# FFN openings put in another order, and the banks of the down units copied out by ScalarE before VectorE adds them to the residual

## The chip, the cores and the metric

The kernel runs on one core of one Trainium2 chip. The metric is the device time of one execution in microseconds, the median of several runs. The engines are named as the profile names them: PE is TensorE (PEld its weight loads), DVE is VectorE, ACT is ScalarE, POOL is GpSimd, and SP is the queue that issues the weight transfers.

## What is computed

One encoder layer over 256 tokens of width 2048, in float32. Two feed-forward blocks (FFN1, FFN2, hidden width 5632) stand around a mixing block, and a small gated embedding and a last norm follow. The change touches the two feed-forward blocks only.

```python
def _rmsnorm(x, g):
    y = x32 * lax.rsqrt(jnp.mean(x32 * x32, axis=-1, keepdims=True) + RMS_EPS)
    return (y * g.astype(jnp.float32)).astype(x.dtype)
def _swiglu(x, wg, wu, wd):
    return (jax.nn.silu(x @ wg) * (x @ wu)) @ wd
...
  h = h + 1/2 * SwiGLU_1(RMSNorm(h))
  (mixing block: attention and short convolution, one output projection)
  h = h + 1/2 * SwiGLU_2(RMSNorm(h))
  h = h + sigmoid(RMSNorm(h) @ W_gate) * (p @ W_ple)
out = RMSNorm(h)
```

## The kernel before, in words

**Pieces.** The residual `h` lies in two token tiles of 128 rows. Weights come in pieces of 128 x 1024 floats, one transfer of 512 KB each on SP, into six `raw` buffers. Each piece is split into two parts whose sum is the weight: ACT writes `whi` (line 109, shown as L45, the line of the helper `act`), DVE writes `wlo` (line 110). Six such pairs of buffers exist (`HELD`, line 93). A product of two such split numbers is three matmuls (L114 to L116), so a piece is 12 matmuls of 128 x 512. A **unit** is the output of 512 columns for both token tiles: two banks of the accumulator memory under the tag `mm`. There are two `mm` banks, so the next such unit can start only when both banks of the unit before have been read out. In the down projection of the first hidden chunk (`down(0, 1, ...)`, names `d0_0` to `d0_3`) a unit is 2 pieces; in the later ones it is 4.

**Gate, up, down.** The hidden width is cut into 11 chunks of 512. `g0` and `u0` are gate and up of the first chunk, done with plain pieces. The other ten gate chunks are done in five **pairs** (`Pair`, names `ffn1s0` to `ffn1s4`) by a product scheme with seven products in place of eight. A pair has 12 steps. In steps 0 to 7 DVE first makes three sums of weights (L347 to L349) and then two pieces are split; steps 8 to 11 make two sums (L358) and split three pieces. The activation side of the scheme comes from `factors`: four small additions on DVE (L317 to L320, `sv`), a rounding on ACT (`sh`) and a difference on DVE (L322, `sl`), one call for each of 4 x 2 groups of 256 rows. After step 11 `whole` (line 402) copies one accumulator on ACT (`x`) and makes six sums on DVE (L405 to L410). `silu` on ACT, `after` (products with the up part on DVE, L486 and for pair 0 also L490) and `turn` (eight transposes on PE, names `gT1`, `gT2`, whose results ACT and DVE split again into `g1h`, `g1l`) follow through a queue.

**What sets the order.** `drive` writes the instructions of every engine in program order, and this order is kept. An item is a piece or a step. Its preparation (transfer, sums, split) is written up to six pieces ahead of its matmuls. `queue` holds deferred work, and `pump` writes one entry of it after each plain piece. `plain_stream` gives the plain pieces: `u0`, `u1`, `u2`, the four units of `down(0, ...)`, then `down` of two chunks and `ups` of two chunks in turn. `everything` puts the steps of the pairs between plain pieces: `at` (lines 556 and 563) says after how many plain pieces each of the 12 steps of pair 0 stands, and `base` where the later pairs begin. In `opening` FFN1 still lacks its `factors`, and calls one for each piece of `u0`; FFN2 has half of them and queues the other four, and its `rstd` behind them.

**The lines of the change.** `run` in `unit_items` (line 158) writes the matmuls, pumps one entry and then, at a unit's last piece, calls `done`. In `down` (line 511) `done` adds both banks, halved, to `h` on DVE (L516). In `up0` FFN1's `done` computes `rstd` (reduction at L225), applies it on ACT, and multiplies on DVE (L448, `gated`). In FFN2 the gate itself stays in the two `mm` banks until ACT's `ffn2sg` has read it.

## Time and profile before

| | |
|---|---|
| median of 3 runs | 1963.72 us (1963.34 to 1965.5) |
| profiled execution: its own time | 1965.0 us |
| its span, and mean granted clock of TensorE | 1962.9 us, 0.989 |
| busy: PE, DVE, ACT, POOL | 1910.3, 1473.9, 1056.6, 35.7 us |
| DMA | 437.09 MB, 65.7% of 16 engines' span |

The span is what the profiler covers of an execution, and the execution's own time stands 2.1 us above it. "Busy" is the share of time in which an engine has an instruction under way. A wait is a stretch in which an engine stands still until a semaphore comes from elsewhere. The granted clock is the share of its full speed that TensorE is given (its levels are 2.4 and 1.2 GHz, so 0.5 is the lower one). A timeline row gives the start, the duration, the engine, the line, the operation with its output and input, and in brackets how long the engine had been idle and what released it.

### The profile page before, as it was taken

What the parts mean: (1) busy time and instruction counts of PE and PEld (TensorE: products, weight loads), DVE (VectorE), ACT (ScalarE), POOL (GpSimd) and SP (SyncE); (2) the same over time, 40 slices, a digit from 0 to 9 for tenths busy, and PEclk for the clock granted to TensorE, in tenths of its full rate; (3) what the DMA queues carried; (4) which work ended last, traced back from release to release, by engine and by line L of the source; (5) the groups of instructions that cost most, each with busy time, mean ns of one, the idle gap of its engine ahead of it and who ended that gap; (6) DMA issues with size and microseconds to landing.
All of it is one profiled execution on the core that took longest, in us unless ns stands there. A gap on an engine that the chain in (4) does not pass through costs nothing.

```text
span 1962.9 us, 23890 instructions
## 1 busy us (share of the span) xinstructions
PE 1910.3 (97%) x8649; PEld 1578.6 (80%) x8649; DVE 1473.9 (75%) x1712; ACT 1056.6 (54%) x1345; POOL 35.7 (2%) x36
## 2 busy tenths in 40 slices
PE   8898999999999999999999989989999999999998
PEld 6686888888888888888888868868888888888887
DVE  6877978879788765656656668778797887987664
ACT  7554555555555555555445555545555555555653
POOL 0000000000000000100000000000000000000010
PEclk9998999999999999999999999989999999999999
DMA  8575776777767765555555547747777667777652
GB/s 293 196 259 186 265 265 225 264 251 245 266 223 240 270 201 183 192 172 165 177 190 177 187 163 230 273 163 260 253 244 271 222 239 268 240 269 238 204 182 99
DMA packets 127206, 437.09 MB, mean 223 GB/s; under 512 B 13808, under 2 KB 14320, under 8 KB 126832
## 3 DMA queue, kind: packets, MB, share of 16 engines
q1 hardware_dynamic: 127088, 435.57, 65.7%
q8 instruction: 68, 1.11, 0.2%
q14 instruction: 50, 0.41, 0.1%
HBM read 433.41 MB, written 2.10 MB: 222 GB/s over the span
## 4 chain that ended last, share of the span: by engine, by line
PE 92%; DVE 3%; ACT 3%; issue 1%; DMA 1%; POOL 0%; ACTq 0%; SPq 0%; POOLq 0%; DVEq 0%
PE ffn2u L114 4%; PE ffn2u L116 4%; PE ffn2u L115 4%; PE ffn1d L114 4%; PE ffn2d L114 4%; PE ffn1d L116 4%; PE ffn1d L115 4%; PE ffn2d L116 4%; PE ffn2d L115 4%; PE ffn1u L114 4%; PE ffn1u L116 4%; PE ffn1u L115 4%; PE o L114 1%; PE o L116 1%; PE o L115 1%; PE pg L116 1%
## 5 line engine op out<-in xcount | busy, mean ns | idle before, releaser
L45 ACT ACTIVATE whi_ffn1s<-raw_ffn1s 128x1024 fp32r<-128x1024 f32 x120 | 126.2, 1061 | 169.6 <-DVE raw_ffn1s L347 38.0
L45 ACT ACTIVATE whi_ffn2s<-raw_ffn2s 128x1024 fp32r<-128x1024 f32 x120 | 126.0, 1061 | 165.3 <-DVE raw_ffn2s L347 39.7
L110 DVE TENSOR_TENSOR wlo_ffn2s<-raw_ffn2s,whi_ffn2s 128x1024 fp32r<-128x1024 f32 x120 | 144.6, 1221 | 14.0 <-ACT whi_ffn2s L45 9.7
L110 DVE TENSOR_TENSOR wlo_ffn1s<-raw_ffn1s,whi_ffn1s 128x1024 fp32r<-128x1024 f32 x120 | 144.7, 1221 | 11.1 <-ACT whi_ffn1s L45 6.5
L114 PE MATMUL ffn2u<-whi_ffn2u,aTh 128*128 128x512 f32 x352 | 138.5, 393 | 7.4 <-ACT ffn2sg L45 7.4
L114 PE MATMUL ffn1u<-whi_ffn1u,aTh 128*128 128x512 f32 x352 | 139.3, 396 | 5.7 <-DVE ffn1sg L448 3.4
L115 PE MATMUL ffn1u<-wlo_ffn1u,aTh 128*128 128x512 f32 x352 | 138.7, 394 | 4.0 <-DVE wlo_ffn1u L110 4.0
L110 DVE TENSOR_TENSOR wlo_ffn2u<-raw_ffn2u,whi_ffn2u 128x1024 fp32r<-128x1024 f32 x88 | 106.0, 1221 | 43.6 <-ACT whi_ffn2u L45 42.4
L116 PE MATMUL ffn1u<-whi_ffn1u,aTl 128*128 128x512 f32 x352 | 138.1, 392 | 0.0
L115 PE MATMUL ffn2u<-wlo_ffn2u,aTh 128*128 128x512 f32 x352 | 137.7, 391 | 0.0
L116 PE MATMUL ffn2u<-whi_ffn2u,aTl 128*128 128x512 f32 x352 | 137.7, 391 | 0.0
L110 DVE TENSOR_TENSOR wlo_ffn1u<-raw_ffn1u,whi_ffn1u 128x1024 fp32r<-128x1024 f32 x88 | 105.7, 1221 | 38.2 <-ACT whi_ffn1u L45 37.2
L45 ACT ACTIVATE whi_ffn2u<-raw_ffn2u 128x1024 fp32r<-128x1024 f32 x88 | 91.1, 1055 | 63.9 <-PE ffn2u L116 45.0
L110 DVE TENSOR_TENSOR wlo_ffn2d<-raw_ffn2d,whi_ffn2d 128x1024 fp32r<-128x1024 f32 x88 | 104.9, 1219 | 17.4 <-ACT whi_ffn2d L45 17.2
L45 ACT ACTIVATE whi_ffn1u<-raw_ffn1u 128x1024 fp32r<-128x1024 f32 x88 | 90.7, 1054 | 50.5 <-PE ffn1u L116 40.8
L110 DVE TENSOR_TENSOR wlo_ffn1d<-raw_ffn1d,whi_ffn1d 128x1024 fp32r<-128x1024 f32 x88 | 104.7, 1220 | 12.4 <-ACT whi_ffn1d L45 12.0
L45 ACT ACTIVATE whi_ffn2d<-raw_ffn2d 128x1024 fp32r<-128x1024 f32 x88 | 89.3, 1048 | 16.3 <-PE ffn2d L116 8.0
L45 ACT ACTIVATE whi_ffn1d<-raw_ffn1d 128x1024 fp32r<-128x1024 f32 x88 | 89.2, 1048 | 11.3 <-PE ffn1d L116 5.1
L114 PEld LDWEIGHTS ffn1u<-whi_ffn1u,aTh 128*128 128x128 f32 x352 | 66.6, 189 | 21.9 <-ACT whi_ffn1u L45 4.4
L114 PEld LDWEIGHTS ffn2u<-whi_ffn2u,aTh 128*128 128x128 f32 x352 | 66.6, 189 | 21.4 <-ACT ffn2sg L45 7.8
L115 PEld LDWEIGHTS ffn1u<-wlo_ffn1u,aTh 128*128 128x128 f32 x352 | 66.8, 190 | 19.6 <-DVE wlo_ffn1u L110 6.0
L116 PEld LDWEIGHTS ffn1u<-whi_ffn1u,aTl 128*128 128x128 f32 x352 | 66.7, 189 | 13.8
(809 smaller groups left out, 5108.9 us busy)
## 6 DMA issues: line engine op xcount, KB each, us to landing
raw_ffn1s<-in_ws SPq DMA_DIRECT2D x120, 512.0 KB, 5.5
raw_ffn2s<-in_ws SPq DMA_DIRECT2D x120, 512.0 KB, 5.4
raw_ffn1u<-in_wu SPq DMA_DIRECT2D x88, 512.0 KB, 5.1
raw_ffn1d<-in_wd SPq DMA_DIRECT2D x88, 512.0 KB, 4.9
raw_ffn2u<-in_wu SPq DMA_DIRECT2D x88, 512.0 KB, 5.1
raw_ffn2d<-in_wd SPq DMA_DIRECT2D x88, 512.0 KB, 4.8
raw_o<-in_wout SPq DMA_DIRECT2D x32, 512.0 KB, 4.5
raw_pg<-in_wpg SPq DMA_DIRECT2D x24, 512.0 KB, 4.6
```

Of the source, the lines that this page charges most:

```text
L45: nc.scalar.activation(out=out, in_=in_, func=func, **kw)
L110: tt(out=lo[:, sl], in0=raw[:, sl], in1=f(hi[:, sl]), op=ALU.subtract)
L114: nc.tensor.matmul(ps, lhsT=xh, rhs=wh, start=first, stop=False)
L115: nc.tensor.matmul(ps, lhsT=xh, rhs=wl, start=False, stop=False)
L116: nc.tensor.matmul(ps, lhsT=xl, rhs=wh, start=False, stop=last)
```

## The change

`down` no longer adds from the banks, except in the last chunk: ACT copies each bank into a work tile (`o`), and the addition on DVE goes into a list `soon`, which `run` empties after the matmuls of the next plain piece, ahead of `done` and of the pumped entry. `done` now comes before the pump, and the number of entries to pump is fixed before it. In all 20 units of each feed-forward block are copied, 80 copies of 128 x 512. FFN1's eight `factors` are spread over `u0` and `u1`, one for every second piece. Both tables `at` are new. The queue entry between `after` and `turn` is left out for FFN1's pair 0, and the second half of `after` of pair 0 becomes an entry of its own. In FFN2 `rstd` stands ahead of the four `factors` in the queue.

```diff
@@ -116,6 +116,7 @@
         nc.tensor.matmul(ps, lhsT=xl, rhs=wh, start=False, stop=last)
 
     queue = deque()
+    soon = []
 
     def pump(n=1):
         for _ in range(min(n, len(queue))):
@@ -162,9 +163,12 @@
                 banks["wide"] = wide
                 st["ps"] = unit_ps(name, wide)
             products(st["ps"], lhs[g], 2 * s, wt, g * 4 + 2 * s, ng * 4 - 1)
-            pump()
+            while soon:
+                soon.pop()()
+            due = min(1, len(queue))
             if g == ng - 1 and s == 1:
                 done(st["ps"])
+            pump(due)
 
         for g in range(ng):
             for s in range(2):
@@ -413,7 +417,8 @@
                 for z in self.c[2 * t:2 * t + 2]:
                     act(z, z, AF.Silu, scale=self.gate["rstd"][:, t:t + 1])
 
-            queue.extend([lambda: (silu(0), silu(1)), self.after, lambda: None, self.turn])
+            queue.extend([lambda: (silu(0), silu(1)), self.after]
+                         + [lambda: None] * self.gap + [self.turn])
 
     def swiglu(nm, nxt, wg, ws, wu, wd, first):
         gate = {}
@@ -456,13 +461,13 @@
                 queue.append(turned(g0, 0, sets))
             return unit_items(wu, 0, f"{nm}u0", aT, done, late=late)
 
-        def up_a(fc, pr, sets):
+        def up_a(fc, pr, sets, late=None):
             def done(pu):
                 ua = [wk(f"{nm}ua{fc}_{t}") for t in range(2)]
                 for t in range(2):
                     act(ua[t], pu[t], scale=gate["rstd"][:, t:t + 1])
                 pr.ua = ua
-            return unit_items(wu, fc, f"{nm}u{fc}", aT, done)
+            return unit_items(wu, fc, f"{nm}u{fc}", aT, done, late=late)
 
         def up_b(fc, pr, sets):
             def done(pu):
@@ -480,15 +485,19 @@
         def pair(i):
             pr = Pair(nm, ws, i, gate)
             pr.sets = []
+            pr.gap = 0 if first and i == 0 else 1
+
+            def after_b():
+                for t in range(2):
+                    tt(out=pr.c[2 * t + 1], in0=pr.ub[t], in1=pr.c[2 * t + 1], op=ALU.mult)
+                queue.append(turned([pr.c[1], pr.c[3]], 2, pr.sets))
 
             def after():
                 for t in range(2):
                     tt(out=pr.c[2 * t], in0=pr.ua[t], in1=pr.c[2 * t], op=ALU.mult)
                 pr.turn_a = turned([pr.c[0], pr.c[2]], 1 + 2 * i, pr.sets)
                 if i == 0:
-                    for t in range(2):
-                        tt(out=pr.c[2 * t + 1], in0=pr.ub[t], in1=pr.c[2 * t + 1], op=ALU.mult)
-                    queue.append(turned([pr.c[1], pr.c[3]], 2, pr.sets))
+                    queue.append(after_b)
 
             pr.after = after
             pr.turn = lambda: pr.turn_a()
@@ -511,11 +520,19 @@
         def down(c0, n, sets, last, wide=False):
             for c in range(4):
                 def done(po, c=c):
-                    for t in range(2):
-                        hs = h[t][:, c * 512:(c + 1) * 512]
-                        stt(out=hs, in0=po[t], scalar=0.5, in1=hs, op0=ALU.mult, op1=ALU.add)
+                    out = [wk(f"{nm}o{c0}_{c}_{t}") for t in range(2)] if not last else po
+
+                    def add():
+                        for t in range(2):
+                            hs = h[t][:, c * 512:(c + 1) * 512]
+                            stt(out=hs, in0=out[t], scalar=0.5, in1=hs, op0=ALU.mult, op1=ALU.add)
                     if last:
+                        add()
                         finish_chunk(nxt, c)
+                    else:
+                        for t in range(2):
+                            act(out[t], po[t])
+                        soon.append(add)
                 yield from unit_items(wd[:, c0:c0 + n], c, f"{nm}d{c0}_{c}", Lazy(sets, n), done,
                                       wide=wide)
 
@@ -525,12 +542,18 @@
                 def late(g, s):
                     if s == 0:
                         load_x(g)
-                    factors(nm, g, s)
+                        factors(nm, g // 2, g % 2)
+
+                def later(g, s):
+                    if s == 0:
+                        factors(nm, 2 + g // 2, g % 2)
                 yield from up0(sets, late)
+                yield from up_a(1, pr, pr.sets, later)
+                yield from up_b(2, pr, pr.sets)
             else:
                 yield from gate0()
                 yield from up0(sets)
-            yield from ups(0, pr)
+                yield from ups(0, pr)
             yield from down(0, 1, sets, False)
 
         def plain_stream(prs):
@@ -553,14 +576,14 @@
         def everything():
             if first:
                 yield from gate0(early)
-                at = [8, 10, 12, 14, 16, 18, 20, 21, 23, 24, 26, 28]
+                at = [8, 10, 12, 14, 16, 18, 20, 22, 24, 26, 28, 29]
                 base = 32
             else:
+                queue.append(lambda: gate.update(rstd=rstd_of(nm)))
                 for c in (2, 3):
                     for p in range(2):
                         queue.append(partial(factors, nm, c, p))
-                queue.append(lambda: gate.update(rstd=rstd_of(nm)))
-                at = [8, 11, 14, 16, 19, 22, 24, 26, 29, 32, 34, 36]
+                at = [8, 10, 13, 16, 18, 20, 22, 24, 26, 28, 30, 32]
                 base = 40
             prs = [pair(i) for i in range(5)]
             places = list(at)
```

**ScalarE in FFN1's `u0`.** `sh0` and `sh1` are the roundings of `factors`, `whi_ffn1u0_g_s` are pieces of `u0`, `junk` the squares for the norm. Before:

```order
L45 ACTIVATE ffn1sh0_286<-ffn1sv0_0_288 128x4x128
L45 ACTIVATE whi_ffn1u0_0_1_309<-raw_ffn1u0_0_1_307 128x1024
L45 ACTIVATE ffn1sh0_286<-ffn1sv0_1_313 128x4x128
L45 ACTIVATE whi_ffn1u0_1_0_334<-raw_ffn1u0_1_0_332 128x1024
L45 ACTIVATE junk_ffn1_0_0_340,ss_ffn1_0_339<-h0_94 128x512
...
L45 ACTIVATE ffn1sh1_348<-ffn1sv1_0_350 128x4x128
L45 ACTIVATE whi_ffn1u0_1_1_371<-raw_ffn1u0_1_1_369 128x1024
L45 ACTIVATE ffn1sh1_348<-ffn1sv1_1_375 128x4x128
L45 ACTIVATE whi_ffn1u0_2_0_396<-raw_ffn1u0_2_0_394 128x1024
```

Now:

```order
L45 ACTIVATE ffn1sh0_286<-ffn1sv0_0_288 128x4x128
L45 ACTIVATE whi_ffn1u0_0_1_309<-raw_ffn1u0_0_1_307 128x1024
L45 ACTIVATE whi_ffn1u0_1_0_327<-raw_ffn1u0_1_0_325 128x1024
L45 ACTIVATE junk_ffn1_0_0_333,ss_ffn1_0_332<-h0_94 128x512
...
L45 ACTIVATE ffn1sh0_286<-ffn1sv0_1_341 128x4x128
L45 ACTIVATE whi_ffn1u0_1_1_362<-raw_ffn1u0_1_1_360 128x1024
L45 ACTIVATE whi_ffn1u0_2_0_380<-raw_ffn1u0_2_0_378 128x1024
```

A rounding stood between any two pieces, and now stands between every second; `sh1` has moved behind the pieces of `u0_2_0`.

**ScalarE after the last step of pair 0 in FFN2.** `x` and `c0` to `c3` belong to `whole` and `silu`, `d0_2`, `d0_3` are units of the first down, `s1_0` the first step of pair 1, `g1h` follows the first transposes. Before:

```order
L45 ACTIVATE ffn2s0x_10337<-ffn2s0q1_10064 128x512
L45 ACTIVATE whi_ffn2d0_3_0_1_10347<-raw_ffn2d0_3_0_1_10345 128x1024
L45 ACTIVATE whi_ffn2s1_0_0_10358<-raw_ffn2s1_0_0_10351 128x1024
L45 ACTIVATE whi_ffn2s1_0_1_10362<-raw_ffn2s1_0_1_10353 128x1024
L45 ACTIVATE ffn2s0c0_9982<-ffn2s0c0_9982,rstd_ffn2_None_9403 128x512
L45 ACTIVATE ffn2s0c1_9983<-ffn2s0c1_9983,rstd_ffn2_None_9403 128x512
L45 ACTIVATE ffn2s0c2_9984<-ffn2s0c2_9984,rstd_ffn2_None_9403 128x512
L45 ACTIVATE ffn2s0c3_9985<-ffn2s0c3_9985,rstd_ffn2_None_9403 128x512
L45 ACTIVATE whi_ffn2d1_0_0_0_10386<-raw_ffn2d1_0_0_0_10384 128x1024
L45 ACTIVATE whi_ffn2d1_0_0_1_10414<-raw_ffn2d1_0_0_1_10412 128x1024
L45 ACTIVATE ffn2g1h_10404<-ffn2gT1_0_10444 128x512
```

Now:

```order
L45 ACTIVATE whi_ffn2d0_2_0_1_10359<-raw_ffn2d0_2_0_1_10357 128x1024
L45 ACTIVATE ffn2s0c0_10018<-ffn2s0c0_10018,rstd_ffn2_None_9376 128x512
L45 ACTIVATE ffn2s0c1_10019<-ffn2s0c1_10019,rstd_ffn2_None_9376 128x512
L45 ACTIVATE ffn2s0c2_10020<-ffn2s0c2_10020,rstd_ffn2_None_9376 128x512
L45 ACTIVATE ffn2s0c3_10021<-ffn2s0c3_10021,rstd_ffn2_None_9376 128x512
L45 ACTIVATE whi_ffn2d0_3_0_0_10383<-raw_ffn2d0_3_0_0_10381 128x1024
L45 ACTIVATE ffn2o0_0_0_10399<-ffn2d0_0_0_10363 128x512
L45 ACTIVATE ffn2o0_0_1_10400<-ffn2d0_0_1_10364 128x512
L45 ACTIVATE whi_ffn2d0_3_0_1_10409<-raw_ffn2d0_3_0_1_10407 128x1024
L45 ACTIVATE ffn2o0_1_0_10441<-ffn2d0_1_0_10413 128x512
L45 ACTIVATE ffn2o0_1_1_10442<-ffn2d0_1_1_10414 128x512
L45 ACTIVATE ffn2g1h_10405<-ffn2gT1_0_10445 128x512
```

All eight pieces of the first down stand behind step 11 now (before, four of them), the pieces of `s1_0` behind the transposes, and the copies `o0_0` and `o0_1` stand in ACT's row behind the four `silu`.

**VectorE at the same place in FFN1.** `c0` to `c3` take the products with `ua` and `ub`, `h` takes the residual. Before:

```order
L110 TENSOR_TENSOR wlo_ffn1d1_0_0_0_1430<-raw_ffn1d1_0_0_0_1427,whi_ffn1d1_0_0_0_1429 128x1024
L486 TENSOR_TENSOR ffn1s0c0_1073<-ffn1ua1_0_884,ffn1s0c0_1073 128x512
L486 TENSOR_TENSOR ffn1s0c2_1075<-ffn1ua1_1_885,ffn1s0c2_1075 128x512
L490 TENSOR_TENSOR ffn1s0c1_1074<-ffn1ub2_0_1196,ffn1s0c1_1074 128x512
L490 TENSOR_TENSOR ffn1s0c3_1076<-ffn1ub2_1_1197,ffn1s0c3_1076 128x512
L516 SCALAR_TENSOR_TENSOR h0_94<-ffn1d0_2_0_1409,h0_94 128x512
L516 SCALAR_TENSOR_TENSOR h1_95<-ffn1d0_2_1_1410,h1_95 128x512
L110 TENSOR_TENSOR wlo_ffn1d1_0_0_1_1458<-raw_ffn1d1_0_0_1_1455,whi_ffn1d1_0_0_1_1457 128x1024
L204 TENSOR_TENSOR ffn1g1l_1448<-ffn1gT1_0_1487,ffn1g1h_1447 128x512
```

Now:

```order
L528 SCALAR_TENSOR_TENSOR h0_94<-ffn1o0_2_0_1449,h0_94 128x512
L528 SCALAR_TENSOR_TENSOR h1_95<-ffn1o0_2_1_1450,h1_95 128x512
L497 TENSOR_TENSOR ffn1s0c0_1091<-ffn1ua1_0_884,ffn1s0c0_1091 128x512
L497 TENSOR_TENSOR ffn1s0c2_1093<-ffn1ua1_1_885,ffn1s0c2_1093 128x512
L208 TENSOR_TENSOR ffn1g1l_1482<-ffn1gT1_0_1499,ffn1g1h_1481 128x512
...
L110 TENSOR_TENSOR wlo_ffn1d1_0_1_1_1553<-raw_ffn1d1_0_1_1_1550,whi_ffn1d1_0_1_1_1552 128x1024
L528 SCALAR_TENSOR_TENSOR h0_94<-ffn1o0_3_0_1495,h0_94 128x512
L528 SCALAR_TENSOR_TENSOR h1_95<-ffn1o0_3_1_1496,h1_95 128x512
L492 TENSOR_TENSOR ffn1s0c1_1092<-ffn1ub2_0_1155,ffn1s0c1_1092 128x512
L492 TENSOR_TENSOR ffn1s0c3_1094<-ffn1ub2_1_1156,ffn1s0c3_1094 128x512
```

The products with `ub` stood directly ahead of the addition from the banks of `d0_2`. They now come after the sums and splits of step `s1_1` (left out at the dots), and the addition reads `o0_2`.

## Rows read from the trace of the kernel before

**Rows 1.** page of the profile, part 1: busy time, share of the span, instructions

```profile
PE 1910.3 (97%) x8649; PEld 1578.6 (80%) x8649; DVE 1473.9 (75%) x1712; ACT 1056.6 (54%) x1345; POOL 35.7 (2%) x36
```

**Rows 2.** waits of PE: engine, its line, what it waited for, us, times, longest

```profile
PE ffn1d L114 <- DVE h L516: 9.6, 1, 9.6
...
PE ffn2d L114 <- DVE h L516: 9.6, 1, 9.6
...
PE ffn2u L114 <- ACT ffn2sg L45: 7.4, 1, 7.4
...
PE ffn1u L115 <- DVE wlo_ffn1u L110: 4.0, 6, 0.8
```

**Rows 3.** windows: us, busy (instructions) by engine, granted clock, DMA share, GB/s

```profile
37.00:73.00 36.00, 24.00 (x85) 15.96 (x85) 26.53 (x48) 19.16 (x33) 3.39 (x3) 0.95 0.45 149
...
73.00:105.10 32.10, 32.10 (x140) 26.52 (x141) 30.20 (x34) 17.68 (x19) 0.00 (x0) 0.95 0.76 263
...
180.00:188.00 8.00, 7.82 (x24) 6.25 (x25) 1.77 (x3) 0.00 (x0) 0.00 (x0) 0.68 0.21 66
...
200.00:240.00 40.00, 40.00 (x178) 33.10 (x178) 37.05 (x42) 20.10 (x20) 0.00 (x0) 1.00 0.81 268
```

**Rows 4.** timeline of DVE, FFN1's `u0`: start, duration, line, operation, idle before

```profile
40.33 1.23 DVE L110 TENSOR_TENSOR wlo_ffn1u<-raw_ffn1u,whi_ffn1u 128x1024 fp32r<-128x1024 f32 x1 [0.26 <-ACT whi_ffn1u L45]
...
41.47 0.28 DVE L317 TENSOR_TENSOR ffn1sv<-a 128x128 f32<-128x128 f32 x1
...
44.26 1.23 DVE L110 TENSOR_TENSOR wlo_ffn1u<-raw_ffn1u,whi_ffn1u 128x1024 fp32r<-128x1024 f32 x1 [0.26 <-ACT whi_ffn1u L45]
...
50.71 1.38 DVE L317 TENSOR_TENSOR ffn1sv<-a 128x128 f32<-128x128 f32 x1
...
52.01 1.36 DVE L318 TENSOR_TENSOR ffn1sv<-a 128x128 f32<-128x128 f32 x1
```

**Rows 5.** timeline of DVE, end of `u0` and the stage of `u1`

```profile
69.91 0.21 DVE L225 TENSOR_REDUCE sm_ffn_None<-ss_ffn 128x1 f32<-128x4 f32 x2
...
71.98 1.41 DVE L448 SCALAR_TENSOR_TENSOR ffn1sg<-ffn1u,rstd_ffn_None,ffn1sg 128x512 f32<-128x512 f32 x2 [1.65 <-ACT ffn1sg L45]
...
81.31 0.68 DVE L347 TENSOR_TENSOR raw_ffn1s<-raw_ffn1s,raw_ffn1s 128x512 f32<-128x512 f32 x1
...
88.12 0.68 DVE L347 TENSOR_TENSOR raw_ffn1s<-raw_ffn1s,raw_ffn1s 128x512 f32<-128x512 f32 x1
```

**Rows 6.** timeline of ACT, FFN2, gate to `u0`

```profile
1157.21 1.28 ACT L45 ACT_TABLE_LOAD   x1
...
1159.56 1.27 ACT L45 ACTIVATE ffn2sg<-ffn2g,rstd_ffn_None 128x512 f32<-128x512 f32 x2 [1.07 <-POOL rstd_ffn_None L231]
```

**Rows 7.** timeline of PE, FFN1's first down, from the end of step 11

```profile
165.02 0.39 PE L114 MATMUL ffn1d<-whi_ffn1d,ffn1g0h 128*128 128x512 f32 x1
...
170.23 0.39 PE L116 MATMUL ffn1d<-whi_ffn1d,ffn1g0l 128*128 128x512 f32 x1
...
180.18 0.76 PE L114 MATMUL ffn1d<-whi_ffn1d,ffn1g0h 128*128 128x512 f32 x1 [9.56 <-DVE h L516]
```

**Rows 8.** timeline of DVE, the same place

```profile
163.81 0.69 DVE L405 TENSOR_TENSOR ffn1s0c<-ffn1s0c,ffn1s0x 128x512 f32<-128x512 f32 x1 [0.30 <-ACT ffn1s0x L45]
...
169.01 0.68 DVE L347 TENSOR_TENSOR raw_ffn1s<-raw_ffn1s,raw_ffn1s 128x512 f32<-128x512 f32 x1
...
176.95 1.28 DVE L486 TENSOR_TENSOR ffn1s0c<-ffn1ua,ffn1s0c 128x512 f32<-128x512 f32 x2
...
179.35 1.28 DVE L516 SCALAR_TENSOR_TENSOR h<-ffn1d,h 128x512 f32<-128x512 f32 x2
```

**Rows 9.** timeline of ACT, the same place and the first transpose after it

```profile
169.86 1.06 ACT L45 ACTIVATE whi_ffn1s<-raw_ffn1s 128x1024 fp32r<-128x1024 f32 x1 [5.14 <-DVE raw_ffn1s L347]
...
172.28 2.54 ACT L45 ACTIVATE ffn1s0c<-ffn1s0c,rstd_ffn_None 128x512 f32<-128x512 f32 x4
...
188.72 1.09 ACT L45 ACTIVATE ffn1g1h<-ffn1gT 128x512 fp32r<-128x512 f32 x2 [12.00 <-PE ffn1gT L292]
```

## The prediction

> **What bounds the kernel.** I read the busy times first. PE has work under way in 1910.3 us, 97% of the span, DVE in 75%, ACT in 54% [rows 1]: matmuls bound the kernel, and this change takes away none of them. What it can win is time in which PE stands still or runs at its lower clock, so the list of PE's waits comes next. All its long waits lie in the openings of the two feed-forward blocks: 9.6 us in each first down on the addition L516, 7.4 us in FFN2 between gate and `u0`, and 4.0 us in six pieces on `wlo` [rows 2]. Between 200 and 240 us there is no loss to win: PE is busy for all 40.00 us at clock 1.00 [rows 3]. So I took the openings one by one. A matmul costs (170.23 - 165.02) / 23 = 0.227 us at full clock [rows 7], a piece of twelve 2.72 us. FFN1's `u0` loses most: between 37 and 73 us only 85 matmuls ran [rows 3], 19.3 us of work in 36.
>
> **A. FFN1's opening.** Before, each piece of `u0` has one `factors`. Its additions on DVE wait for the piece's `wlo`, the rounding on ACT waits for them, and the next `whi` waits behind the rounding, so `wlo` comes every 44.26 - 40.33 = 3.93 us [rows 4] where PE takes 2.72. The change leaves four of the eight there. Two pieces then cost 3.93 + 1.23 (a plain `wlo`) = 5.2 us against 5.44 of PE, and PE should keep up. Taking the step's 12 matmuls and the one at the end from the 85, 72 belong to `u0`; it would end at 37 + 72 x 0.227 = 53.3 us, its last `wlo` near 50.3. From there DVE needs the sums and splits of step 0 (the 6.81 us of a step's cycle [rows 5] less two plain splits, about 4.5), two splits and one factor (5.2): the reduction starts near 60, not at 69.91 [rows 5]. The product L448 stands 2.07 us behind it, and PE follows when the first half of that is done, 0.8 later. `u1` then starts near 62.8 instead of 72.8, where the second stretch of [rows 3] begins: 10.0 us gained.
>
> The other four factors must be paid in `u1`. There DVE's cycle per step is 88.12 - 81.31 = 6.81 us [rows 5], with a factor 6.81 + (3.93 - 1.23) = 9.5, while PE needs three times 2.72 = 8.2. Three such cycles, the start of 0.6, the split of `g0` (1.3) and 3.3 to the split of step 4 make 33.9 us from the start of `u1` to step 4; PE needed 32.1 before [rows 3]. That gives back 1.8. Then GpSimd: DVE's L317 once took 1.38 us and the L318 behind it 1.36, against 0.28 elsewhere [rows 4], in the stretch where POOL is busy for 3.39 us [rows 3]. In the new order such an overlap may fall on the way to L448 and cost up to 2.2 more. I take half of it, since no row says when the transfer behind POOL's work will land: 10.0 - 1.8 - 1.1, **7.1 us gained**. At 9 the overlap misses; at 4 it costs all and one more cycle of 3.93 is paid by half.
>
> **B. FFN2, gate to `u0`.** PE waits for `ffn2sg`, which had to wait 1.07 us for `rstd` after the table load of 1.28 [rows 6]. With `rstd` first that wait goes. But four factors with 3.93 us each still run ahead of the table load, and they bind next: **1.1 gained**. It is 0 if they end as late as `rstd` did, and 2 if a plain `whi` moves behind `ffn2sg` too.
>
> **C. FFN1's first down.** Call T the end of step 11 (165.02 before). The chain to the banks is now: six sums from T - 1.2, a split, the sums of the next step at T + 4.0 [rows 8], whose `whi` is behind them on ACT [rows 9], silu 2.54, then products with `ua` and `ub` at 1.28 each, then L516 at T + 14.3. PE waited from T + 5.4 to T + 15.2 and then ran 24 matmuls in 7.8 us instead of 5.4, the clock being 0.68 [rows 3]. After the change the copies take the place of L516; what they wait for on ACT is the two `whi` of step `s1_0`. One less split stands ahead (one piece of `d2` is behind step 11), so the second `whi` ends near T + 6.2, one more `whi` at T + 7.1, and the copies free the first bank at T + 7.7. PE had no work since T + 2.7: 5.1 us instead of 9.6, and I let the lost clock (2.4) stand. A new wait comes for it. The products with `ub` are queued on DVE behind the sums and splits of `s1_1` (6.8) and the second addition, so the second transposes come about 2.5 us late. 4.5 - 2.5 = 2.0, and 0.9 with one more `whi` (1.06) ahead of the copies: **1.2 gained**. It is -1 if both stops grow by that, and 4 if the clock recovers sooner.
>
> **D. FFN2's first down.** Here all eight pieces of `d0` stand behind step 11, 21.8 us of PE's work as cover. Silu ends near T + 6.1, one `whi` later the copies of the first unit begin, and its first bank is free at T + 7.8, where PE has been done since T + 5.4: 2.5 us lost. The second unit's copies begin as it ends and cost 0.3 behind the transposes. The third stop is the one of C: the sums of `s1_0` wait for the split of the transposes (T + 16.6), and the `ub` products end at T + 23.7, where PE had `d2` ready until T + 20.3: 3.1 lost. Together 5.9 us, where before 9.6 were waited and 2.4 lost on the clock. That is 6.1 less; short stops may lower the clock too, so I take off half of one such loss: **4.9 gained**. At 1 both stops lose the clock in full; at 7 the `ub` products come 1 us earlier.
>
> **E. The 80 copies.** A pair of ACT's copies out of accumulator banks takes 1.09 us [rows 9], so 40 pairs add 44 us to ACT's 1056.6. Eight pairs lie in C and D. The others have a step of a pair between two units, at least 2.72 us of PE's work while the copies need 1.1, and ACT is busy only 20.10 of 40 us there [rows 3]. That step is the cover; without it each unit boundary would cost 1.1 us or more. DVE gains nothing in work: a pair of additions from the banks takes 1.28 us, and a pair of the products L486, which read no bank, 1.28 too [rows 8]. I cost E at 0.
>
> **The sum.** 7.1 + 1.1 + 1.2 + 4.9 = 14.3 us. The profiled execution took 1965.0 us, so 1950.7; the median of the runs is 1.3 below the profiled one, so 1949.4. The ends of the four terms add up to 4 and 22.
>
> **Rivals.** (1) *The stops do not shorten as replayed*: DVE stays the bound of `u1`, clock losses follow each of the two new stops in C and D. 4 + 0.5 - 1 + 1.5 = 5 us: 1958.7. For it speaks that DVE has work in 30.20 of 32.1 us in that stage already [rows 3].
>
> (2) *The clock holds over the shorter stops.* C and D gain 2 each more, A's upper end holds: 20 us, 1943.7. For it speaks clock 0.95 between 37 and 73 us, where PE stood still often but briefly [rows 3].
>
> (3) *The wait only moves.* If the `ub` products and the bank copies give back C and D whole, and POOL's overlap and DVE eat A, 1 us is left: 1962.7. Against it speaks that PE's missing work between 37 and 73 us is the largest loss and has a plain cause.
>
> (4) *Slower: the bank is freed later everywhere.* In 32 units outside the openings DVE's addition freed the banks; now ACT must, in order, behind `whi` that themselves wait for DVE's sums. It decides from the point where the copies end later than 2.72 us after the unit's last matmul. At 1 us beyond that in each, 32 us lost against 14.3 gained: 1981.4. Against it: ACT is half idle there and prepares pieces six ahead. A rule of the Trainium skill speaks for this one in kind (VectorE: DVE Perf Modes, Rules for kernel authors): on a matmul's output, either take DVE's slow rate from the accumulator or copy it out first "if you'll do many ops". Here one operation follows each copy. The trace agrees that the copy buys DVE no speed (1.28 us a pair either way); by the rule E is pure cost, and by the rows it is a cost under cover.
>
> **How the numbers follow.** The forecast as summed has 0.60, rival 1 0.17, rival 2 0.10, rival 3 0.07, rival 4 0.06. Under 0.2%, 3.9 us, a measurement cannot be told from no change. Faster by more: the forecast, rival 2 and most of rival 1, 0.85; same 0.09; slower 0.06. With not all terms at one end the forecast's own range is 1944 to 1957; with rivals 1 and 2 it becomes 1942 to 1960.
>
> **What would show it.** Right: PE dense from 31 to 53 us, `u1` starting at 61 to 66, step 4 of pair 0 near 97 to 100; the two waits of 9.6 replaced by one near 5 (FFN1) and by one of 2 to 3 (FFN2), both on ACT's `o`, and two of 2 to 4 us on the `ub` products; `ffn2sg` wait near 6; PE without waits from 200 us on. Wrong: waits of PE on `o` copies in the later units (rival 4), pieces of `u1` that wait for `wlo` by more than 3 us a step (rival 1), or waits on the transposes as long as those on L516 were (rival 3).

## The result, and the profile after

The changed kernel takes **1949.33 us** (median of 3 runs, 1948.67 to 1950.84) against 1963.72: a ratio of 0.9926, 95% interval 0.9903 to 0.9948. A second set of runs of the same kernel gave 1949.61 and 0.9921 (0.9906 to 0.9935); its profile is called the second profile below, and the first one "after". The profiled execution's span is 1947.0 us where it was 1962.9, at mean clock 0.991. The forecast was 1949.4.

The busy times after, as in [rows 1]:

```profile
PE 1907.2 (98%) x8649; PEld 1578.5 (81%) x8649; DVE 1468.5 (75%) x1712; ACT 1094.9 (56%) x1425; POOL 35.5 (2%) x36
```

PE's 8649 matmuls are the same, so the 15.9 us of span are idle time (12.8 us) and stretched matmuls (3.1 us of busy time) that went away. PE's waits, to be laid beside [rows 2] (engine, line, what was waited for: us in total, times, longest):

```profile
PE ffn1u L114 <- DVE ffn1sg L453: 8.3, 1, 8.3
PE ffn2u L114 <- ACT ffn2sg L45: 6.2, 1, 6.2
PE ffn1d L114 <- ACT ffn1o L45: 5.0, 1, 5.0
...
PE ffn2gT L296 <- DVE ffn2s0c L492: 2.7, 2, 2.5
PE ffn1gT L296 <- DVE ffn1s0c L492: 2.2, 2, 1.9
...
PE ffn2d L114 <- ACT ffn2o L45: 0.9, 1, 0.9
```

Both waits of 9.6 us on the additions are gone. ACT's copies `o` stand there with 5.0 and 0.9, and the products with `ub` (now L492) hold the second transposes by 2.2 and 2.7 us. The first line is one stop of 8.3 us behind `u0` (the product L453, once L448). Before, PE stood there for 3.4 us, after many small stops like the six on `wlo` in [rows 2]:

```profile
PE ffn1u L114 <- DVE ffn1sg L448: 3.4, 1, 3.4
```

To see which stretch gained what, I cut each trace at five of PE's instructions: the first matmul of `u0`, of step 4 of pair 0, of the third step of FFN1's pair 1, of FFN2's `u0`, and of the third step of FFN2's pair 1. Each stretch between two cuts holds the same work in all kernels. "Rest" is from the last cut to the last matmul.

| us | before | after | gained | forecast | gained in the second profile |
|---|---|---|---|---|---|
| start to `u0` | 31.24 | 30.93 | 0.3 | 0 | -0.7 |
| A: `u0` to step 4 | 73.94 | 66.19 | **7.75** | 7.1 | 8.2 |
| C: step 4 to FFN1's third step of pair 1 | 101.00 | 100.80 | **0.2** | 1.2 | 1.5 |
| B: from there to FFN2's `u0` | 954.12 | 953.00 | **1.1** | 1.1 | 1.1 |
| D: `u0` to FFN2's third step of pair 1 | 155.49 | 149.06 | **6.4** | 4.9 | 5.4 |
| rest | 637.37 | 637.37 | 0.0 | 0 | 0.0 |

The gains sum to 15.8 us, and to 15.5 in the second profile; 14.3 were forecast. The steady part of both blocks, the mixing block and the tail contribute nothing.

One profile fixes the gains of C and D only roughly. Seven profiles below have FFN1's two stops as in after (4.99 us, and 1.94 to 2.08), and C takes 99.03 to 101.59 us in them; six have FFN2's (0.93 or 0.94, and 2.52 or 2.53), and D takes 147.59 to 151.19. Against the one profile of the kernel before, C gained -0.6 to 2.0 us and D 4.3 to 7.9. The waits repeat far better than these totals, so where an edit's effect is small, I go by the waits.

**Opening of FFN1.** Stretches of after (columns as in [rows 3]; the last row belongs to FFN2's opening):

```profile
37.00:53.00 16.00, 16.00 (x72) 13.24 (x72) 12.64 (x20) 11.04 (x19) 0.00 (x0) 1.00 0.64 224
64.00:97.10 33.10, 33.10 (x140) 27.12 (x141) 29.37 (x43) 16.41 (x19) 0.00 (x0) 0.93 0.57 190
200.00:240.00 40.00, 40.00 (x178) 33.14 (x177) 34.40 (x38) 20.53 (x23) 0.00 (x0) 1.00 0.80 262
1250.00:1300.00 50.00, 46.34 (x204) 37.59 (x204) 37.66 (x47) 26.79 (x36) 0.00 (x0) 0.97 0.51 175
```

The 72 matmuls of the first row are done by 53 us with PE dense and at clock 1.00; before, 85 took 36 us. Then PE stops once, until `u1` at 63.85. What DVE does in that stop (start, duration, line, operation; in brackets the idle time and what ended it), and in a step cycle of `u1` that holds a factor:

```profile
49.27 0.68 DVE L351 TENSOR_TENSOR raw_ffn1s<-raw_ffn1s,raw_ffn1s 128x512 f32<-128x512 f32 x1
...
53.73 2.34 DVE L110 TENSOR_TENSOR wlo_ffn1u<-raw_ffn1u,whi_ffn1u 128x1024 fp32r<-128x1024 f32 x1
56.00 1.35 DVE L321 TENSOR_TENSOR ffn1sv<-a 128x128 f32<-128x128 f32 x1
57.27 0.28 DVE L322 TENSOR_TENSOR ffn1sv<-a 128x128 f32<-128x128 f32 x1
...
60.98 0.21 DVE L229 TENSOR_REDUCE sm_ffn_None<-ss_ffn 128x1 f32<-128x4 f32 x2
...
63.04 1.41 DVE L453 SCALAR_TENSOR_TENSOR ffn1sg<-ffn1u,rstd_ffn_None,ffn1sg 128x512 f32<-128x512 f32 x2 [1.65 <-ACT ffn1sg L45]
...
84.77 0.69 DVE L351 TENSOR_TENSOR raw_ffn1s<-raw_ffn1s,raw_ffn1s 128x512 f32<-128x512 f32 x1
...
94.38 0.68 DVE L351 TENSOR_TENSOR raw_ffn1s<-raw_ffn1s,raw_ffn1s 128x512 f32<-128x512 f32 x1
```

POOL in the same stretch:

```profile
53.70 3.49 POOL L684 TENSOR_TENSOR bm<-bm,msk 128x512 f32<-128x512 f32 x2 [52.37 <-DMA bm<-in_bias]
```

The split at 53.73 takes 2.34 us instead of 1.23, the factor's first addition 1.35 instead of 0.28, while POOL does its two operations. The cycle from 84.77 to 94.38 is 9.61 us.

**Openings of the down projections.** PE's stops there, and ACT in FFN2:

```profile
168.13 0.80 PE L114 MATMUL ffn1d<-whi_ffn1d,ffn1g0h 128*128 128x512 f32 x1 [4.99 <-ACT ffn1o L45]
...
186.80 0.30 PE L296 MATMUL ffn1gT<-ident,ffn1s0c 128*128 128x128 f32 x1 [1.94 <-DVE ffn1s0c L492]
...
1260.65 0.50 PE L114 MATMUL ffn2d<-whi_ffn2d,ffn2g0h 128*128 128x512 f32 x1 [0.93 <-ACT ffn2o L45]
...
1275.24 0.30 PE L296 MATMUL ffn2gT<-ident,ffn2s0c 128*128 128x128 f32 x1 [2.52 <-DVE ffn2s0c L492]
```

```profile
1255.62 0.71 ACT L45 ACTIVATE ffn2s0c<-ffn2s0c,rstd_ffn_None 128x512 f32<-128x512 f32 x1
1257.22 1.95 ACT L45 ACTIVATE ffn2s0c<-ffn2s0c,rstd_ffn_None 128x512 f32<-128x512 f32 x3 [0.89 <-DVE ffn2s0c L414]
...
1260.02 1.06 ACT L45 ACTIVATE ffn2o<-ffn2d 128x512 f32<-128x512 f32 x2
```

So the first unit's banks are freed from 1260.02 on, and PE has lost 0.93 us where 9.6 stood.

### The profile page after: what moved, and what is told of

The parts are those of the page before. It is cut to its first block, busy times and chain, and to the rows that moved or that the text cites. A ratio compares the mean times of both kernels' runs of the same rounds, so it can differ in the third digit from the quotient of the medians.

```text
span 1947.0 us, 23939 instructions
## 1 busy us (share of the span) xinstructions
PE 1907.2 (98%) x8649; PEld 1578.5 (81%) x8649; DVE 1468.5 (75%) x1712; ACT 1094.9 (56%) x1425; POOL 35.5 (2%) x36
## 4 chain that ended last, share of the span: by engine, by line
PE 90%; DVE 3%; ACT 2%; issue 1%; ACTq 0%; POOLq 0%; POOL 0%; DVEq 0%
PE ffn2u L114 4%; PE ffn2u L116 4%; PE ffn2u L115 4%; PE ffn2d L114 4%; PE ffn2d L116 4%; PE ffn2d L115 4%; PE ffn1d L114 4%; PE ffn1d L116 4%; PE ffn1d L115 4%; PE ffn1u L115 3%; PE ffn1u L116 3%; PE ffn1u L114 3%; PE o L116 1%; PE o L114 1%; PE o L115 1%; PE pg L116 1%
```

## Experiments

Each kernel is the changed kernel with one edit, if nothing else is said. Kernels measured together share a "before": 1965.04 us for the first four, 1965.36 for the next three and the second set of the changed kernel, 1963.93 for the last four. The ratios are to it.

**1. Copies in the first chunk only.** Asks whether the other 64 copies cost or earn anything (rival 4).

```diff
-out = [wk(f"{nm}o{c0}_{c}_{t}") for t in range(2)] if not last else po
+out = [wk(f"{nm}o{c0}_{c}_{t}") for t in range(2)] if c0 == 0 else po
```
(for `c0 > 0`, `add()` reads the banks at once)

> Copies on ACT are kept for the four units of the first down of each feed-forward block; in the 32 later units DVE adds from the banks at once, as before the change. My theory (the copies in the later units lie under a step of the pair): same as the changed kernel, 1949 +- 2 us, no waits of PE after the openings, ACT's busy time 35 us less. Rival (the copies delay the banks everywhere): faster by 5 us or more, about 1944. Second rival (the copies free banks sooner everywhere and earn the gain): slower by 5 us or more, and PE waits on the additions in the later units.

Measured: 1952.19 us, 0.9934 (0.9919 to 0.9949), span 1949.5. That is just outside the theory's 1949 +- 2. A, B and C are inside the spread of the changed kernel's two profiles or within 0.6 us of it. D takes 151.19, 1.1 to 2.1 more, with the same stops and a lower clock (199 matmuls at 0.93 from 1250 to 1300 us, where after has 204 at 0.97); whether that belongs to the edit, no run shows. One wait is new, behind the last cut of FFN2:

```profile
PE ffn2d L114 <- DVE h L528: 0.8, 1, 0.8
```

At that boundary the addition stood behind two splits on DVE, and 1.07 us were lost in the stretch after it. No other unit outside the openings shows a wait. So no trace shows a cost of the 64 later copies, and one wait that they saved. Of the 2.6 to 2.9 us by which this kernel is slower, that explains 1.1.

**2. No copies at all.**

```diff
-out = [wk(f"{nm}o{c0}_{c}_{t}") for t in range(2)] if not last else po
+out = po
...
+add()
...
-for t in range(2):
-    act(out[t], po[t])
-soon.append(add)
```

> No copies at all: DVE adds from the banks, directly at the end of each unit and ahead of the pumped entry; all the rest of the change stays. My theory: only the first downs lose. In FFN1 the addition stands behind the splits of the next step on DVE and frees the bank near 1.7 us later than the copy did; in FFN2 the first unit's addition comes behind the splits of the pieces ahead, about 1.8 us later, with little more at the next two stops. In sum slower than the changed kernel by 3 to 6 us, 1952 to 1955. Rival (the order of FFN2's steps and of the queue earns the first downs' gain, the copies nothing): 1949 +- 1.5. Rival (the copies are what gains in general): 1957 or more.

Measured: 1952.01 us, 0.9934 (0.9919 to 0.9948), span 1948.8. PE's waits:

```profile
PE ffn1d L114 <- DVE h L528: 6.5, 1, 6.5
...
PE ffn2d L114 <- DVE h L528: 4.7, 3, 2.8
...
PE ffn1gT L296 <- DVE ffn1s0c L492: 1.0, 2, 0.8
```

In FFN1 the first stop grows by 1.5 us and the second shrinks by 1.1: C takes 99.00 us, no longer than with copies. In FFN2 D takes 152.05; its stops are 6.0 us in place of 3.5. By the medians all 80 copies together earn 2.4 to 2.7 us, which the intervals of the ratios do not tell apart, and experiment 1, which keeps the copies of the first downs, takes as long (1952.19). By PE's waits the copies earn 2.5 us in FFN2's first down and 0.3 in FFN1's.

**3. FFN1's factors back.** All eight on the pieces of `u0`, as before.

```diff
-factors(nm, g // 2, g % 2)
+factors(nm, g, s)
...
-yield from up_a(1, pr, pr.sets, later)
+yield from up_a(1, pr, pr.sets)
```

> FFN1's eight factors go back to one for each piece of u0; the changed table and all else stay. My theory: the opening gives back what it gained, 7.8 us (step 4 of pair 0 starts at 97.1 us now and would start near 105 again): 1957. Rival (the new places of the steps and the order of the queue gained it): 1949 to 1951.

Measured: 1956.63 us, 0.9959 (0.9944 to 0.9974), span 1953.2. `u1` starts at 72.76 and step 4 at 105.32, where before had 72.78 and 105.18: the whole of A is the spread of the factors. The same profile shows something else. In FFN2's opening, with the same stops as after (0.94 and 2.52), the clock held; this is the counterpart of the last row of after's stretches, where it was 0.97:

```profile
1258.00:1308.00 50.00, 46.33 (x211) 37.81 (x211) 39.47 (x49) 28.37 (x39) 0.00 (x0) 1.00 0.53 183
```

211 matmuls ran instead of 204, 7 x 0.227 = 1.6 us, and D takes 147.59 instead of 149.06.

**4. The `ub` products with the `ua` products**, the transposes left where they are. Asks whether the `ub` products' place is the second stop.

```diff
 def after_b():
-    for t in range(2):
-        tt(out=pr.c[2 * t + 1], in0=pr.ub[t], in1=pr.c[2 * t + 1], op=ALU.mult)
...
 if i == 0:
+    for t in range(2):
+        tt(out=pr.c[2 * t + 1], in0=pr.ub[t], in1=pr.c[2 * t + 1], op=ALU.mult)
     queue.append(after_b)
```

> The products with ub come directly behind those with ua on DVE, in both blocks; the entry that writes the second transposes keeps its place. My theory (the second stop of each first down is these products, queued behind a step's sums and splits): PE's waits on the second transposes (2.2 us in FFN1, 2.7 in FFN2) go, and with them the matmuls at the lower clock behind them (about 1.5 and 1.7 us): 8 us faster than the changed kernel, 1941. Rival (the products only move the wait: the splits behind the first transposes and with them step 1 of pair 1 come 1.3 us later, or the second transposes wait for something else): 1947 to 1950.

Measured: 1942.88 us, 0.9887 (0.987 to 0.9903), span 1940.9. DVE takes the products right behind each other, and PE does the second transposes of FFN2 without a wait:

```profile
174.94 1.29 DVE L495 TENSOR_TENSOR ffn1s0c<-ffn1ua,ffn1s0c 128x512 f32<-128x512 f32 x2
176.15 1.29 DVE L499 TENSOR_TENSOR ffn1s0c<-ffn1ub,ffn1s0c 128x512 f32<-128x512 f32 x2
```

```profile
1270.88 1.03 PE L296 MATMUL ffn2gT<-ident,ffn2s0c 128*128 128x128 f32 x8
```

C is 97.18 (99.50 to 100.80 with the changed kernel) and D 145.77 (149.06 to 150.08). The entry of its own that the change gave these products cost 6 to 7 us, a little less than the theory's 8: the waits of 2.2 and 2.7 us, and the clock behind them.

**5. FFN2's old table `at`.** The work tiles `wk` go from 10 to 11 buffers, which that order needs.

```diff
-WK = 10
+WK = 11
...
-at = [8, 10, 13, 16, 18, 20, 22, 24, 26, 28, 30, 32]
+at = [8, 11, 14, 16, 19, 22, 24, 26, 29, 32, 34, 36]
```

> FFN2's table goes back to the one before the change (four, not eight, pieces of the first down behind step 11), and the ring of work tiles gets one more buffer, without which this order would block itself. My theory (the cover behind step 11 is what shortened FFN2's first stop; the copies had little part, since without them 2 to 3 us were lost): FFN2's first down loses again near what FFN1's does, a wait of about 5 us on the copies and one of 2 on the transposes, so 4 to 6 us slower than the changed kernel. Rival (the copies shortened it): within 1.5 us of the changed kernel.

Measured: 1956.54 us, 0.9955 (0.994 to 0.997), span 1955.4.

```profile
PE ffn2u L114 <- ACT ffn2sg L45: 7.2, 1, 7.2
PE ffn2d L114 <- ACT ffn2o L45: 5.8, 1, 5.8
```

D takes 154.72 us, 0.8 less than before, and the gate's wait is 7.2. The first stop is 5.76 us in place of 0.93 and the second 2.08 in place of 2.52, so the table, with its eight pieces of `d0` behind step 11, carries 4.4 us of D's gain in waits, and 4.6 to 5.7 by the totals of the changed kernel's two profiles. The eleventh buffer was not tried by itself. B loses 0.9, so the table is in B too.

**6. FFN2's `rstd` behind the factors again.**

```diff
-queue.append(lambda: gate.update(rstd=rstd_of(nm)))
 for c in (2, 3):
     for p in range(2):
         queue.append(partial(factors, nm, c, p))
+queue.append(lambda: gate.update(rstd=rstd_of(nm)))
```

> FFN2's rstd goes back behind the four factors in the queue. My theory: PE's wait on the gate is 7.4 us again instead of 6.2, 1.1 us slower than the changed kernel, which only the trace can show. Rival (the wait is bound by the factors alone): 6.2 us again.

Measured: 1950.98 us, 0.9927 (0.991 to 0.9943); the wait on `ffn2sg` is 6.8 us, and B 953.61. `rstd`'s place is worth 0.6 of the 1.1, half of what the theory said, and the new table 0.9 to 1.0 (experiment 5, where `rstd` stands first and the wait is 7.2 all the same). The two overlap and do not add; why the table moves this wait was not followed up.

**7. As 4, and FFN1's `rstd` in the seventh of `u0`'s eight pieces**, ahead of DVE's last splits.

```diff
 def silu0():
-    if first:
-        gate["rstd"] = rstd_of(nm)
...
 def late(g, s):
     if s == 0:
         load_x(g)
         factors(nm, g // 2, g % 2)
+    if g == 3 and s == 0:
+        gate["rstd"] = rstd_of(nm)
```

> As the run with the ub products moved, and FFN1's rstd is computed while u0 is still prepared. My theory (u1's stage is bound by DVE from its first product on, and DVE stood idle 1.65 us for rstd and the gate on ACT): u1 starts 1.7 to 2.0 us earlier, and so does step 4: 1.7 to 2.0 us faster than the run with the ub products alone. Rival (DVE takes the same work later and PE waits within u1 instead): no gain at step 4.

Measured: 1940.17 us, 0.9873 (0.9858 to 0.9887), span 1937.2. `u1` starts at 62.25, step 4 at 95.58, 2.2 us ahead of experiment 4. That repeats: `u1` starts at 63.85 to 64.72 in the eight profiles with the spread factors and `rstd` in its old place, and at 61.88 to 62.51 in the four with this edit. The stop behind `u0` is 6.1 us, not 8.3: part of it was the chain reduction, `rstd`, silu, product in a row.

**8. The later units' banks copied four times.** The forecast had priced rival 4 only by an assumed overrun; here it is made.

```diff
 for t in range(2):
-    act(out[t], po[t])
+    for _ in range(4 if c0 else 1):
+        act(out[t], po[t])
```

> The changed kernel, but each bank of the 32 later units is copied four times in place of once, all into the same work tile: a unit's copies take about 4.4 us, where the step of the pair that covers them takes 2.7. My theory (a copy costs nothing up to the length of that step, and what lies beyond it is paid): PE waits 4.4 + 0.3 - 2.9 = about 1.8 us at each of the 32 boundaries, less where steps 8 to 11 (4.1 us) stand there: 45 to 60 us slower than the changed kernel. Rival (the queue behind the copies on ACT is the price, not the banks): more than 80 us slower, with PE's waits on whi and wlo. Rival (boundaries have more cover than a step): under 10 us.

Measured: 1984.83 us, 1.0101 (1.0083 to 1.0119), span 1982.9, 35.9 over after. PE's waits, and one boundary on ACT and on PE:

```profile
PE ffn1d L114 <- ACT ffn1o L45: 15.6, 13, 5.0
PE ffn2d L114 <- ACT ffn2o L45: 12.8, 14, 1.4
```

```profile
215.62 4.87 ACT L45 ACTIVATE ffn1o<-ffn1d 128x512 f32<-128x512 f32 x8 [0.71 <-PE ffn1d L116]
```

```profile
220.54 0.50 PE L114 MATMUL ffn1d<-whi_ffn1d,ffn1g1h 128*128 128x512 f32 x1 [0.88 <-ACT ffn1o L45]
```

The copies end at 220.49 and PE goes on at 220.54, on the unit's second bank: it had started on the first, which is free earlier, with three matmuls, the last at 219.28. Without the wait it would have gone on at 219.28 + 0.23 = 219.5, and the copies began at 215.62, just before the step's matmuls. A pair of copies thus has 3.9 us of cover here, and 4.87 is 1.0 too much. That fits the mean price, 35.9 / 32 = 1.1 us a boundary. The expectation had put the price too high, since it left out the first bank and let all eight copies start later. Rival 4's mechanism is there, and only its condition is not met: a pair of copies takes 1.1 of the 3.9 us.

**9. As 7, and FFN1's end packed as FFN2's**: more pieces of `d0` behind step 11 as cover.

```diff
-pr.gap = 0 if first and i == 0 else 1
+pr.gap = 1
...
-at = [8, 10, 12, 14, 16, 18, 20, 22, 24, 26, 28, 29]
+at = [8, 10, 12, 14, 16, 17, 19, 20, 21, 22, 23, 24]
```

> As the run with the ub products and rstd moved, and FFN1's steps stand closer, so that step 11 comes before all eight pieces of the first down, as in FFN2 (table 8, 10, 12, 14, 16, 17, 19, 20, 21, 22, 23, 24, and the empty queue entry of pair 0 is back). My theory (cover behind step 11 is what shortens the stop): FFN1's wait of 5.0 us falls to about 1 and its lowered clock goes too, 6 us; one plain piece a step leaves DVE 5.7 us of work to 5.4 of PE over a few steps and gives back about 1: 4 to 6 us faster than that run. Rival (DVE in the stage of the close steps takes it all back): within 1.5 us.

Measured: 1939.25 us, 0.987 (0.9853 to 0.9888), span 1937.2, the same as 7, so the rival's "within 1.5 us" came.

```profile
PE ffn1u L114 <- ACT ffn1ua L45: 3.5, 1, 3.5
...
PE ffn1d L114 <- ACT ffn1o L45: 0.9, 1, 0.9
```

```profile
99.09 1.06 ACT L45 ACTIVATE whi_ffn1s<-raw_ffn1s 128x1024 fp32r<-128x1024 f32 x1 [2.21 <-DVE raw_ffn1s L351]
100.54 1.06 ACT L45 ACTIVATE whi_ffn1s<-raw_ffn1s 128x1024 fp32r<-128x1024 f32 x1 [0.40 <-DVE raw_ffn1s L353]
101.51 1.25 ACT L45 ACTIVATE ffn1ua<-ffn1u,rstd_ffn_None 128x512 f32<-128x512 f32 x2
```

The copies' wait falls from 5.0 to 0.9, and 3.5 us come up earlier: `u1`'s banks are read by `ua`, which on ACT stands behind two `whi` of a step that wait for DVE's sums. DVE's backlog moved the stop from one bank to another.

**10. As 7, and four empty entries between FFN2's `rstd` and its four factors**, so that these run behind the gate.

```diff
 queue.append(lambda: gate.update(rstd=rstd_of(nm)))
+queue.extend([lambda: None] * 4)
```

> As the run with the ub products and rstd moved, and in FFN2 the four factors stand four empty entries later in the queue, behind the gate's silu. My theory (ACT's silu of the gate waits in order behind the factors' roundings): PE's wait of 6.2 us between gate and u0 falls to 2 or less; the factors then cost DVE 2.7 us each in the stage of u0, part of which comes back as waits on splits: 3 to 5 us faster than that run. Rival (the factors are paid in full later): within 1.5 us.

Measured: **1933.93 us**, 0.9844 (0.9828 to 0.9859), span 1931.3. ACT ahead of the gate in kernel 7, and then here:

```profile
1138.56 0.63 ACT L45 ACTIVATE ffn2sh<-ffn2sv 128x512 fp32r<-128x512 f32 x1 [2.35 <-DVE ffn2sv L324]
...
1142.48 0.63 ACT L45 ACTIVATE ffn2sh<-ffn2sv 128x512 fp32r<-128x512 f32 x1 [2.35 <-DVE ffn2sv L324]
1143.13 1.28 ACT L45 ACT_TABLE_LOAD   x1
1144.42 1.26 ACT L45 ACTIVATE ffn2sg<-ffn2g,rstd_ffn_None 128x512 f32<-128x512 f32 x2
```

```profile
1135.95 1.28 ACT L45 ACT_TABLE_LOAD   x1 [3.74 <-PE ffn2g L116]
1137.24 1.27 ACT L45 ACTIVATE ffn2sg<-ffn2g,rstd_ffn_None 128x512 f32<-128x512 f32 x2
1138.39 0.63 ACT L45 ACTIVATE ffn2sh<-ffn2sv 128x512 fp32r<-128x512 f32 x1
```

In kernel 7 the roundings `sh`, each waiting 2.35 us for DVE, stand ahead of the gate's silu. Here silu waits only for the gate's last matmul; PE's wait on `ffn2sg` is 0.5 us instead of 6.2, and the span is 5.9 shorter, more than the 3 to 5 expected.

**11. Kernels 9 and 10 together.**

> The two last edits together on the run with the ub products and rstd moved. They lie in different blocks, so my theory expects the sum of their gains: 7 to 11 us faster than that run, 1930 +- 3 where the kernel before takes 1965.

Measured: 1932.86 us, 0.9837 (0.9822 to 0.9853), span 1931.1: 7.3 us faster than 7, just inside the expected 7 to 11, but not as it was reckoned: 6.2 are 10's gain, and 9 alone had given 0.9, within the noise. It is the best of the study by its median, but its interval and 10's overlap nearly whole; either is 0.8% under the changed kernel.

## Why the prediction was right, point by point

**The total** came out within 0.3 us, and that closeness is luck: A and D were too low by 0.7 and 1.5 (1.1 and 0.5 in the second profile), C too high by 1.0 in one profile and too low by 0.3 in the other. The profiles gained 15.8 and 15.5 us, not 14.3; the medians differ by only 14.4, since the kernel before was profiled in an execution 1.3 us above its median and the changed one in an execution at its median. The sets of runs of the kernel before alone differ by 1.6 us in their medians (1963.72 to 1965.36). The mechanisms, not the last digit, are what was right.

**A, right in mechanism and size.** 8.6 us from `u0` to `u1`, 0.9 given back up to step 4. The cycle with a factor took 9.61 us (forecast 9.5), and experiment 3 shows that without the spread all of A is gone. Two terms had a wrong size. The 1.8 given back in `u1` were 0.9: `u1` to step 4 took 33.3 us where 33.9 were forecast, and 32.4 before, where the forecast read 32.1 off a window that starts 0.2 late and ends 0.1 early. The other is the overlap with POOL: half of 2.2 us was taken, and it fell in full, (2.34 - 1.23) + (1.35 - 0.28) = 2.2 on the way to the reduction. That this came at 60.98 all the same means that the rest of the chain was 1.2 us shorter than replayed, mostly because DVE began the sums of step 0 at 49.27 and not at 50.3. The upper end of A does not follow from its own terms either: with no overlap they give 10.0 - 1.8 = 8.2, not 9.

**B, right in size, half right in cause.** The 1.1 us came, and the factors do bind next, as said; but the forecast gave all of it to `rstd`'s place, and experiments 6 and 5 show 0.6 for that and 0.9 to 1.0 for the table, overlapping. That the wait behind it was a matter of ACT's order and worth 5.9 us, experiment 10 shows.

**C, stops right, clock not.** The first stop was 4.99 us (5.1), the second 1.94 (2.5). The waits fell by a good 2 us (9.6 against 5.0 and 2.2), as forecast. The step that failed is "let the lost clock (2.4) stand": there were two stops, and behind the second one the clock may fall again. Behind the first and the second stop of after, and then of the second profile, where both stops end 0.6 and 0.9 us later:

```profile
168.00:176.00 8.00, 7.66 (x28) 5.95 (x29) 4.67 (x6) 5.14 (x9) 0.00 (x0) 0.81 0.75 254
184.50:196.00 11.50, 9.35 (x38) 7.32 (x37) 10.12 (x14) 5.10 (x6) 0.00 (x0) 0.85 0.55 181
```

```profile
168.00:176.00 8.00, 7.31 (x23) 5.88 (x24) 5.06 (x7) 4.53 (x9) 0.00 (x0) 0.67 0.74 245
184.50:196.00 11.50, 9.22 (x44) 7.34 (x44) 10.12 (x14) 5.11 (x6) 0.00 (x0) 1.00 0.55 184
```

After lost clock twice, the second profile once and for longer; from the second stop's end to the cut PE took 11.1 us in the one and 9.5 in the other, and C differs by 1.3. The copies bear little of C: without them the first stop is 6.5 us, still 3.1 under the 9.6 of before, and C is no longer (experiment 2). Which part of the new order bears the 3.1 (FFN1's table, the queue entry left out, `done` ahead of the pump) stays open, as no run takes one of them back by itself.

**D, right in kind, first stop mis-sized.** It was 0.93 us, not 2.5. "Silu ends near T + 6.1" took silu as one piece behind the last of the six sums; its first quarter ran at 1255.62, ahead of that sum, which leaves 1.95 us behind it and not 2.54. Silu ended near T + 5.1 (T is 1254.12 here), and PE went on at T + 6.5 and not at T + 7.8; the quarter explains 0.6 of these 1.3 us, and the rest was not traced. The last stop was 2.52 (3.1). Where the text reckoned with eight pieces as cover and with the copies, it did not say how much each bears. Experiments 5 and 2 do, in waits: the table 4.4 us, the copies 2.5. The stops fell from 9.6 to 3.5, by 6.1, so the two do not simply add; each is measured with the other in place.

**E, right.** The copies' own time was 23.3 us in FFN1 and 22.9 in FFN2, 46 in place of 44, all of it covered. Between 200 and 240 us PE ran 178 matmuls in 40 us as in [rows 3], and experiment 1 finds no cost of the later copies. The sentence on the VectorE page of the Trainium skill (VectorE: DVE Perf Modes, Rules for kernel authors), that made E a pure cost, is about DVE's work; here what counts is when a bank is free, and copying bought that at no price that a trace shows. DVE's additions took 683 ns each from the copies and 686 ns from the banks before, so the copy bought DVE nothing, as forecast.

**The rivals.** Rival 4 was rightly put low: experiment 8 shows its wait and where it begins. Rival 3 did not come. Of rival 1 one half was there, the clock that falls behind both new stops of C (after), but not its price. Rival 2, the clock that holds, is partly in some profiles (D of experiment 3), never in both C and D with these stops. Of the signs named ahead one failed: FFN2's stop on `o` was 0.9 and not 2 to 3. **Not foreseen** was what the change leaves lying: the `ub` products' own entry (6 to 7 us, experiment 4), the roundings ahead of silu (5.9, experiment 10) and the late `rstd` (2.2, experiment 7).

## What to carry to other kernels

Where a buffer holds up the bottleneck engine, look at what stands ahead of its reader in that engine's own queue and what those instructions wait for: here moving two products, one reduction and four empty entries was worth as much as the whole change. In this kernel work on another engine was free as long as it ended inside the piece that covers it; find that point by making the work longer until a wait appears (copies of 1.1 us a pair cost nothing, copies of 4.9 cost 1.1 us a boundary, and the rows put the limit at 3.9), not by its share of busy time. When an order and a copy are changed together, measure each alone, because the sum says nothing about which one bore it.

## What the runs showed of the hardware

Two-input operations on DVE took longer while POOL worked on its two 128x512 tiles: 2.34 us instead of 1.23 for a split of 128x1024, 1.35 instead of 0.28 for an addition of 128x128; before the change 1.38 and 1.36 instead of 0.28 [rows 4]. Each of the four lost 1.1 us whatever its size, two of them beside POOL's two operations in either kernel, so this looks like a fixed stop for each of POOL's operations and not like a lower rate; no run varies POOL's work. The Trainium skill (GPSIMD Engine Reference, Specifications) says that the two engines share their access to SBUF and that DVE's instructions with two SBUF inputs contend; the trace agrees in kind and gives the size for these tiles.

The clock behind a stop of about 2 us is not the same in each execution of the same code: behind the 2.52 us of FFN2's last stop it stayed at 1.00 over 50 us in one kernel (experiment 3), was 0.97 in another (after) and 0.93 in a third (experiment 1). From that stop's end to the third step of pair 1, PE took 23.1, 24.7 and 25.8 us for the same 104 matmuls. In these runs such a stop's price was its own length and up to 2.7 us more, and a stretch of one profile is uncertain by at least that. What decides it, no run here shows.
